# First transfers, second norm and last chunks reordered in a one-core encoder block

## The chip, the core and the metric

The kernel runs on one core of a Trainium2 chip. The metric is device microseconds of one execution. The core's engines run side by side, each in its own order of instructions, and wait for each other by semaphores: TensorE (PE in the profile; its weight loads are PEld), VectorE (DVE), ScalarE (ACT), GpSimd (POOL) and SyncE (SP), which issues nearly all transfers.

## The reference, cut to what matters

One layer over 1024 positions of width 1024, all in float32, with D_FF = 2816:

```python
h = rmsnorm(x, norm1_g);  proj = h @ w_in               # columns: q, k, v of group A, then of group B
ya = chunked_attention(qa, ka, va, rel_bias)            # 8 heads of 64
yb = stick_breaking_attention(qb, kb, vb)               # 8 heads of 64
x = x + concat(rmsnorm(ya, g_a), rmsnorm(yb, g_b)) @ w_out
x = x + conv_gated_mlp(rmsnorm(x, norm2_g), ...)        # up, causal conv of 3, silu(gate) * value, down
return rmsnorm(x, final_g)
```

## The kernel before, in words

Everything is held transposed: a tile is 128 channels by 1024 positions, so x is eight tiles (`KT = 8`), `xT[0]` to `xT[7]`. Every float32 product is made of three matmuls: each operand is split into a high part (rounded, type fp32r, made by ACT as a cast) and a low part (source minus high part, made by DVE or POOL), and `mm3` (L140) multiplies high by high, high by low and low by high. A matmul has at most 512 columns, so a tile is worked in two halves, `lo` and `hi` (`rows(0)`, `rows(1)`).

The order of PE is written out by hand for the whole kernel (`pe_order`). From the first value projection on, the order of SP, DVE, ACT and POOL is the order of the program text too (`loads_order`, `own_order`), partly by way of a small planner with costs (`Flow`). Before that point, the start stage leaves these four to a scheduler.

**Start (L203 to L269, L876 to L889).** Ten warm-up matmuls on zeros; then the first q and k projections (weights `w_in[12]` and `w_in[16]`) of all eight tiles. SP brings q's weights in two halves around the two halves of x's first tile, then x's second tile, k's weights, the other six tiles, and the first two v weights. For each tile, `enter` (L227) makes the scaled high part (`hTh`, ACT) and low part (`hTl`, DVE); `square` (L234) squares the tile in place, odd tiles on POOL, even ones on ACT, and DVE adds the squares into two sums. PE takes q of tile i and then k of tile i-1. The low and high half of a weight tile serve x's tiles 0 to 3 and 4 to 7. The sums are due after five steps of the v projection (`rstd`, `totals`).

**Second norm (L1176 to L1243, L1400 to L1440).** The output projection adds to `x2` (`paf` scales what PE made, L848; L852 adds), half 0 of all tiles and then half 1. While half 1 is made, `second_norm(0)` scales half 0 tile by tile (`scalar_tensor_tensor`, L1207), ACT casts (`h2h`, L1210), and DVE makes the low part (`h2l`). `totals` gives column sums of squares on PE (`n_ms`), `across` spreads them by transposes (`n_rb`). `up_first` then does the up-projection of the first channel tile plainly: sixteen groups of three matmuls on half 0 (`n` counts them), then eight tiles of half 1, two channel tiles each, in the order `K_ORDER[1]`. `norms[1]` is the same generator for half 1, advanced once at n = 5 (the totals) and once in each group from n = 8 (the transposes and the first tile). `weights1` splits the next weights; `combine_all` makes sums and differences of tiles (`t2`, `t3`, `t4`: Strassen-like products later). The bank of `u_a`, the first matmuls of the product for channel tile 3 (L1364), is emptied by an ACT copy at L1503, which stands behind the work for channel tiles 0 and 1 in ACT's order.

```python
if low:
    sub(*low.pop())                  # low part of the tile before
V.scalar_tensor_tensor(out=f, in0=f, scalar=c1(C_G2 + k), in1=ob, op0=ALU.mult, op1=ALU.mult)
S.copy(h, f)
low.append((l, f, h))
```

**Last chunks (`last_down`, L1757 to L1818).** The last two channel tiles of the down-projection are done for three groups of positions: 384, 384 and 256 columns (`LAST`). For each group and each of eight channel tiles: six matmuls (`dnl`), a DVE add into `x2` (L1808), a square (ACT, L1180 or L1185) with a POOL add into an accumulator (L1186). When a group is through, `final` is queued for it: the totals and the reciprocal root (`rn`), its transposes (`n_rb`), an ACT copy for POOL, and then eight scalings, of which POOL does those in `POOLD` or `POOLM` (ACT applies the gain to these beforehand, L1812) and DVE the others (L1783). `go(n)` advances it by n steps from within the next group's loop. The first two groups store each tile on its own (192 KB, L1787); the last one fills `res`, which leaves in two stores of 512 KB (L1818), after which the run ends.

## Time and profile before

| | us |
|---|---|
| median of 3 runs (lowest to highest) | 1247.58 (1245.27 to 1248.05) |
| the profiled execution, its own time | 1247.4 |
| its span, first to last instruction | 1245.6 |
| PE busy in the span | 1221.6 |
| DVE, ACT, POOL busy | 975.6, 633.8, 342.1 |
| granted TensorE clock, mean over the span | 0.994 |

The rows further down are single lines of the profile's views. In the timeline a row holds the start, the time covered, the engine, the line of the kernel, the operation, the tile written and the tiles read, the shape, the count (equal neighbours are merged), and in brackets how long the engine stood idle before it and what it waited for. Tiles of one name with other numbers are not told apart. A busy time of PE says little by itself, since matmuls overlap; the starts of neighbouring matmuls do.

### The profile page before, as it was taken

Reading aid. Unit: us, or ns where it says so; the run is one execution under the profiler, and the core shown is the slowest. Engines: PE = TensorE matmul, PEld = TensorE weight load, DVE = VectorE, ACT = ScalarE, POOL = GpSimd, SP = SyncE. Lnnn points to the kernel's source line nnn. Section 1 sums busy time; section 2 is a strip of 40 time slices with the busy share of each in tenths; the row PEclk is TensorE's granted clock in tenths of the full one; section 3 lists DMA queues with packets and bytes.
Section 4 is the critical chain, followed back from the end, with each engine's and each line's share of the span. In section 5 each row is a group of like instructions: output and inputs, shape, how many; then the busy total and the mean of one; then the engine's idle time right before and its main releaser. Section 6 shows DMA issues by size and latency. Waiting matters only on the chain.

```text
span 1245.6 us, 18039 instructions
## 1 busy us (share of the span) xinstructions
PE 1221.6 (98%) x6936; PEld 1031.8 (83%) x6936; DVE 975.6 (78%) x1403; ACT 633.8 (51%) x1072; POOL 342.1 (27%) x240
## 2 busy tenths in 40 slices
PE   8999999999999999999999999999999999999996
PEld 6989888988898788887778888888888887888886
DVE  7677788687676878557789888788787779969885
ACT  6345766665665756524455444444444445444434
POOL 3220113021312221242003443344344322132034
PEclk8999999999999999999999999999999999999998
DMA  5121122122302281234022212212212196430003
GB/s 223 34 56 31 59 61 93 28 77 77 86 18 60 53 243 69 86 103 151 1 85 102 102 70 83 102 68 85 101 69 85 53 380 243 158 113 1 1 1 135
DMA packets 39749, 113.47 MB, mean 91 GB/s; under 512 B 4720, under 2 KB 7920, under 8 KB 39664
## 3 DMA queue, kind: packets, MB, share of 16 engines
q1 hardware_dynamic: 39520, 112.22, 26.5%
q8 instruction: 54, 0.88, 0.3%
q14 instruction: 31, 0.25, 0.1%
q10 hardware_dynamic: 144, 0.11, 0.0%
HBM read 80.85 MB, written 24.12 MB: 84 GB/s over the span
## 4 chain that ended last, share of the span: by engine, by line
PE 83%; DVE 9%; ACT 4%; issue 2%; POOL 1%; DMA 1%; SPq 0%; DVEq 0%; ACTq 0%; POOLq 0%
PE u_a L1364 8%; PE u_e L1364 8%; PE dz L1879 8%; PE v_p L558 7%; PE q_p L143 6%; PE k_p L143 6%; PE u_c L1364 4%; PE u_b L1364 4%; PE u_d L1364 4%; PE pb L143 3%; PE dm L1879 3%; PE dj L1879 3%; PE pa L143 3%; PE yb L659 2%; PE tpb L645 2%; PE yy L774 2%
## 5 line engine op out<-in xcount | busy, mean ns | idle before, releaser
L622 DVE TENSOR_TENSOR_SCAN zb<-zb,first 128x128 f32<-128x128 f32 (+3 forms) x64 | 86.7, 1360 | 40.9 <-ACT zb L618 40.4
L558 PE MATMUL v_p<-v_h,hTh 128*128 128x256 f32 x256 | 74.2, 290 | 0.7 <-DVE k_f L435 0.7
L1388 DVE SCALAR_TENSOR_TENSOR gt<-cg,cst,gt 128x1023 f32<-128x1023 f32 (+1 forms) x44 | 74.0, 1681 | 0.8
L558 PE MATMUL v_p<-v_l,hTh 128*128 128x256 f32 x256 | 72.3, 283 | 0.0
L558 PE MATMUL v_p<-v_h,hTl 128*128 128x256 f32 x256 | 72.3, 282 | 0.0
L1254 POOL TENSOR_TENSOR up_r<-up_r 128x512 f32<-128x512 f32 x18 | 39.2, 2178 | 103.8 <-issue 92.5
L617 ACT ACTIVATE acts<-zb 128x127 f32<-128x127 f32 (+3 forms) x64 | 42.1, 658 | 43.6 <-PE zb L609 43.2
L649 ACT COPY tb<-tpb 128x512 f32<-128x512 f32 (+3 forms) x96 | 43.5, 483 | 33.2 <-PE tpb L645 32.9
L1388 DVE SCALAR_TENSOR_TENSOR vt<-cv,cst,vt 128x1023 f32<-128x1023 f32 (+1 forms) x44 | 57.7, 1311 | 1.5 <-ACT vt L1382 0.7
L143 PE MATMUL q_p<-hTh,q_h 128*128 128x512 f32 x128 | 53.0, 424 | 2.4 <-ACT hTh L229 2.4
L740 ACT ACTIVATE pa<-sa,sta 128x640 f32<-128x640 f32 (+4 forms) x64 | 42.3, 662 | 22.4 <-DVE sta L726 17.8
L121 POOL TENSOR_TENSOR q_l<-q_r,q_h 128x1024 fp32r<-128x1024 f32 x7 | 16.7, 2391 | 132.8 <-ACT q_h L416 132.8
L143 PE MATMUL k_p<-hTh,k_h 128*128 128x512 f32 x128 | 51.2, 410 | 0.0
L1382 ACT ACTIVATE vt<-cv,cst 128x1024 f32<-128x1024 f32 x22 | 27.4, 1245 | 45.9 <-DVE cv L1257 45.9
L143 PE MATMUL q_p<-hTl,q_h 128*128 128x512 f32 x128 | 49.7, 398 | 0.2
L558 PEld LDWEIGHTS v_p<-v_h,hTh 128*128 128x128 f32 x256 | 48.7, 190 | 1.2 <-DVE k_f L435 0.9
L143 PE MATMUL q_p<-hTh,q_l 128*128 128x512 f32 x128 | 49.3, 396 | 0.0
L143 PE MATMUL k_p<-hTh,k_l 128*128 128x512 f32 x128 | 49.2, 395 | 0.0
L143 PE MATMUL k_p<-hTl,k_h 128*128 128x512 f32 x128 | 49.2, 395 | 0.0
L558 PEld LDWEIGHTS v_p<-v_h,hTl 128*128 128x128 f32 x256 | 48.8, 191 | 0.3
L558 PEld LDWEIGHTS v_p<-v_l,hTh 128*128 128x128 f32 x256 | 48.8, 191 | 0.0
L625 DVE TENSOR_TENSOR acts<-zb,acts 128x127 f32<-128x127 f32 (+3 forms) x64 | 47.4, 749 | 1.2
(1265 smaller groups left out, 4042.2 us busy)
## 6 DMA issues: line engine op xcount, KB each, us to landing
up_r<-in_w_up_dram SPq DMA_DIRECT2D x44, 512.0 KB, 4.4
act<-vt SPq DMA_DIRECT2D x22, 512.0 KB, 2.6
dr<-in_w_dn_dram SPq DMA_DIRECT2D x20, 512.0 KB, 5.8
dr<-act SPq DMA_DIRECT2D x20, 512.0 KB, 6.6
k_r<-in_w_in_dram SPq DMA_DIRECT2D x8, 512.0 KB, 3.6
v_r<-in_w_v_dram SPq DMA_DIRECT2D x8, 512.0 KB, 4.1
spill<-yb SPq DMA_DIRECT2D x16, 256.0 KB, 2.0
wo_r<-in_w_out_dram SPq DMA_DIRECT2D x8, 512.0 KB, 3.7
```

Of the source, the lines that this page charges most:

```text
L143: PE.matmul(o, w[:, sl], t[:, rows(g)], start=first and i == 0, stop=last and i == 2,)
L558: PE.matmul(ov, a[k][:, cols(t)], b[:, sl], start=k == 0 and i == 0 and t4 % 2 == 0, stop=k == KT - 1 and i == 2, skip_group_check=True,)
L617: S.activation(a[:, 1:w], z[:, 1:], AF.Sigmoid)
L622: on_v(2 * w + 70, lambda: V.tensor_tensor_scan(out=z, data0=z, data1=first[:, :w], initial=0.0, op0=ALU.mult, op1=ALU.add)),
L625: on_v(w, lambda: V.tensor_tensor(out=a[:, 1:w], in0=z[:, : w - 1], in1=a[:, 1:w], op=ALU.mult)),
L649: mine.append(flow.add(on_s(m * P, lambda o=o, tp=tp: S.copy(o, tp))))
L740: on_s(w + 170, lambda: S.activation(po, full, AF.Exp, bias=st[:, 0:1], accum_out=st[:, 1:2])),
L1254: eng.tensor_tensor(out=out, in0=a, in1=b, op=ALU.subtract)
L1364: PE.matmul(o, w[:, cols(k)], t, start=start and k == 0 and i == 0, stop=k == 3 and i == 2, skip_group_check=True,)
L1382: S.activation(t, self.c[w], AF.Identity, bias=c1(C_CB + ct), scale=c1(C_W2 + ct))
L1388: V.scalar_tensor_tensor(out=t[:, : T - lag], in0=o[:, lag:], scalar=c1(c + ct), in1=t[:, : T - lag], op0=ALU.mult, op1=ALU.add,)
L1879: PE.matmul(o[m], w[:, cols(m)], t, start=i in (0, 1, 4, 5) and p == ps_[0] and j == 0, stop=p == ps_[-1] and j == 2, skip_group_check=True,)
```

## The change

At the start, transfers and engine work are written in order of first use: both orders by hand (`loads_order`, `own_order`) now begin here; q and k weights both come in halves, k's low half before x's second tile, both high halves behind it; PE takes q and k of the same tile; all squares are ACT's, three tiles late, and DVE's adds four tiles late; the v weights are brought and split before the last squares. In the second norm, the low part of a tile is made after the scaling of the next one, for half 0 and half 1; the steps of half 1 begin at n = 10 in place of 8, what is left of them is emitted ahead of PE's half 1, with the second part of `weights1` and three of the four steps of `combine_all("t2")`, which is a generator now. In the last chunks POOL's tiles are 2; 6 and 7; 2 and 4 for the three groups, the steps of `final` are called later, and the results leave in four stores of 256 KB.

```diff
--- before.py
+++ after.py
@@ -33,8 +33,7 @@
 CHUNKS = (range(5), range(5, 10))
 LAST = ((0, 3), (3, 6), (6, 8))
 ORDER_B = (7, 0, 6, 1, 5, 2, 4, 3)
-POOLD = (2, 6)
-POOLM = (2,)
+POOL_D = {3: (2,), 6: (6, 7), 8: (2, 4)}
 RATE_B, LEAD_B = 31.0, 8.0
 RATES_A, LEAD_A = (25.0, 25.0, 25.0, 21.0), 6.5
 LAG = 0.25
@@ -42,7 +41,8 @@
 SLACK = 0.6
 DRAIN = 1.6
 EARLY = 2
-SQ_LAG = 2
+SQ_LAG = 3
+ADD_LAG = 4
 WARM = 10
 TAIL_A = (6, 8, 4)
 X2_TAGS = ("h1", "l1", "h2", "l2", "x4", "x5", "h0", "l0")
@@ -215,14 +215,23 @@
             return weights(src, name, pool, tags, raw=work(tag, f"{name}_r"), bufs=bufs)
 
         halves = (slice(0, GW), slice(GW, T))
-        raw = work("wa", "q0_r")
-        pre = {12: (wp.tile([P, D], F32R, tag="wh", name="q0_h"), wp.tile([P, D], F32R, tag="wl", name="q0_l"))}
-        t0 = slot(0, "xin0")
-        nc.sync.dma_start(raw[:, halves[0]], w_in[12][:, halves[0]])
-        nc.sync.dma_start(t0[:, halves[0]], xT[0][:, halves[0]])
-        nc.sync.dma_start(t0[:, halves[1]], xT[0][:, halves[1]])
-        nc.sync.dma_start(raw[:, halves[1]], w_in[12][:, halves[1]])
-        hh, hl, sums, xin = [], [], [], []
+        lo, hi = halves
+        loads_order = tc.manual_schedule(engines={nc.sync.engine})
+        loads_order.__enter__()
+        own_order = tc.manual_schedule(engines={V.engine, S.engine, GP.engine})
+        own_order.__enter__()
+        pre, raw = {}, {}
+        for ct, name, tag in ((12, "q0", "wa"), (16, "k0", "wb")):
+            raw[ct] = work(tag, f"{name}_r")
+            pre[ct] = [wp.tile([P, D], F32R, tag=t, name=f"{name}_{t}") for t in ("wh", "wl")]
+        xin = [slot(k, f"xin{k}") for k in range(KT)]
+        hh, hl, sums = [], [], []
+
+        def bring(t, src, r):
+            nc.sync.dma_start(t[:, r], src[:, r])
+
+        def prepare(ct, r):
+            split(*(t[:, r] for t in pre[ct]), raw[ct][:, r])
 
         def enter(k, r):
             a, b, t = hh[k][:, r], hl[k][:, r], xin[k][:, r]
@@ -232,40 +241,50 @@
             )
 
         def square(k):
-            t = xin[k]
-            if k % 2:
-                GP.tensor_tensor(out=t, in0=t, in1=t, op=ALU.mult)
+            S.activation(xin[k], xin[k], AF.Square)
+
+        def add(k):
+            if k < 2:
+                sums.append(xin[k])
             else:
-                S.activation(t, t, AF.Square)
-            if k < 2:
-                sums.append(t)
-            else:
-                V.tensor_tensor(out=sums[k % 2], in0=sums[k % 2], in1=t, op=ALU.add)
-
+                V.tensor_tensor(out=sums[k % 2], in0=sums[k % 2], in1=xin[k], op=ALU.add)
+
+
+        bring(raw[12], w_in[12], lo)
+        bring(xin[0], xT[0], lo)
+        bring(xin[0], xT[0], hi)
+        bring(raw[16], w_in[16], lo)
+        nc.sync.dma_start(xin[1], xT[1])
+        bring(raw[12], w_in[12], hi)
+        bring(raw[16], w_in[16], hi)
+        for k in range(2, KT):
+            nc.sync.dma_start(xin[k], xT[k])
         for k in range(KT):
-            xin.append(slot(k, f"xin{k}") if k else t0)
-            if k:
-                nc.sync.dma_start(xin[k], xT[k])
             a, b = hpair(k, "hT")
             hh.append(a)
             hl.append(b)
             if k == 0:
-                split(pre[12][0][:, halves[0]], pre[12][1][:, halves[0]], raw[:, halves[0]])
-                enter(0, halves[0])
-                enter(0, halves[1])
-                split(pre[12][0][:, halves[1]], pre[12][1][:, halves[1]], raw[:, halves[1]])
+                prepare(12, lo)
+                enter(0, lo)
+                enter(0, hi)
+                prepare(16, lo)
             else:
                 enter(k, slice(0, T))
-            if k == 1:
-                pre[16] = preload(w_in[16], "k0", "wb")
+            if k == 3:
+                prepare(12, hi)
+                prepare(16, hi)
             if k >= SQ_LAG:
                 square(k - SQ_LAG)
+            if k >= ADD_LAG:
+                add(k - ADD_LAG)
+        pre[0] = preload(w_v[0], "v0_0", "wa", kp, ("y1", "y2"), 1)
+        pre[1] = preload(w_v[1], "v0_1", "wb", kp, ("x10", "x11"), 1)
         for k in range(KT - SQ_LAG, KT):
             square(k)
+        for k in range(KT - ADD_LAG, KT):
+            add(k)
         V.tensor_tensor(out=sums[0], in0=sums[0], in1=sums[1], op=ALU.add)
-        tc.keep_in_program_order(S.preload_act_table_set("sqrt_and_others"))
-        pre[0] = preload(w_v[0], "v0_0", "wa", kp, ("y1", "y2"), 1)
-        pre[1] = preload(w_v[1], "v0_1", "wb", kp, ("x10", "x11"), 1)
+        S.preload_act_table_set("sqrt_and_others")
 
         class Chain:
 
@@ -874,17 +893,12 @@
 
 
         oq, ok = (big(f"{w}0_p") for w in "qk")
-        for i in range(KT + 1):
-            for o, ct, k in ((oq, 12, i), (ok, 16, i - 1)):
-                if 0 <= k < KT:
-                    mm3(
-                        [o[:, rows(g)] for g in range(G)], *pre[ct], cols(k), hh[k], hl[k],
-                        k == 0, k == KT - 1,
-                    )
-        loads_order = tc.manual_schedule(engines={nc.sync.engine})
-        loads_order.__enter__()
-        own_order = tc.manual_schedule(engines={V.engine, S.engine, GP.engine})
-        own_order.__enter__()
+        for k in range(KT):
+            for o, ct in ((oq, 12), (ok, 16)):
+                mm3(
+                    [o[:, rows(g)] for g in range(G)], *pre[ct], cols(k), hh[k], hl[k],
+                    k == 0, k == KT - 1,
+                )
         fetch()
         fetch()
         v0 = project_v(0)
@@ -1202,12 +1216,12 @@
                 if g == 0:
                     hp2[k] = hpair(k, "h2", H2_TAGS.get(k))
                 f, (h, l) = x2[k][:, r], (t[:, r] for t in hp2[k])
-                if low:
-                    sub(*low.pop())
                 V.scalar_tensor_tensor(
                     out=f, in0=f, scalar=c1(C_G2 + k), in1=ob, op0=ALU.mult, op1=ALU.mult
                 )
                 S.copy(h, f)
+                if low:
+                    sub(*low.pop())
                 low.append((l, f, h))
                 if i == KT - 1:
                     sub(*low.pop())
@@ -1244,8 +1258,6 @@
     with stage("ffn"):
         fp = pools["sbuf"]
 
-        lo, hi = halves
-
         def at(slot, name, dt=F32):
             pool = wp if slot == "wr" else fp if slot[0] == "s" else cp
             return pool.tile([P, T], dt, tag=slot, name=name, bufs=1)
@@ -1344,6 +1356,7 @@
                 if low:
                     low()
                 low = nxt
+                yield
             low()
 
         def right(what, k):
@@ -1424,17 +1437,22 @@
                     if n == 5:
                         next(norms[1])
                         weights1(0)
-                    if 8 <= n:
+                    if n >= 10:
                         next(norms[1])
                     plain(o[0, ct], up_w[ct], k, 0, k == 0, k == KT - 1)
                     n += 1
                 S.copy(c[0][ct // NF][:, lo], o[0, ct])
+            for _ in norms[1]:
+                pass
+            weights1(1)
+            sums = combine_all("t2")
+            for _ in range(3):
+                next(sums)
             for i, k in enumerate(K_ORDER[1]):
                 for ct in (0, NF):
                     plain(o[1, ct], up_w[ct], k, 1, i == 0, i == KT - 1)
             for ct in (0, NF):
                 S.copy(c[0][ct // NF][:, hi], o[1, ct])
-            weights1(1)
             w2, raws2 = [], up_raw.pop(2)
 
             def weights2(n):
@@ -1453,20 +1471,23 @@
 
             done = Finish(0, *c[0])
             done.first("g")
+            for _ in sums:
+                pass
             done.first("v")
             low = weights2(0)
-            combine_all("t2")
             done.taps("g")
             done.taps("v")
             done.silu()
             low()
             done.gate()
-            combine_all("t3")
+            for _ in combine_all("t3"):
+                pass
             c[1] = (at("s7", "cg1"), at("s8", "cv1"))
             product_1(0, med)
             low = weights2(1)
             load_up(3)
-            combine_all("t4")
+            for _ in combine_all("t4"):
+                pass
             low()
             product_1(1, pj)
             load_up(4)
@@ -1773,8 +1794,8 @@
                 across(ob, rn2, c0, c_end)
                 rb = fp.tile([P, GW], F32, tag="eb", name=f"n3_{c0}_rbs", bufs=1)[:, :n]
                 S.copy(rb, ob)
-                pool_d = POOLD if c_end == KT else POOLM
-                for d in sorted(range(KT), key=lambda d: d not in pool_d):
+                pool_d = POOL_D[c_end]
+                for d in range(KT) if c_end == 6 else sorted(range(KT), key=lambda d: d not in pool_d):
                     x = x2[d][:, sl]
                     y = res[d // 4][:, d % 4, :] if c_end == KT else x
                     if d in pool_d:
@@ -1808,15 +1829,21 @@
                     V.tensor_tensor(out=x2[d][:, sl], in0=x2[d][:, sl], in1=o, op=ALU.add)
                     last = accs[: {3: 1, 6: 2, 8: 4}[c_end]]
                     x2_part(x2, d, sl, [a[:, sl] for a in last], None, f"n3_{c0}", sqs[d % 2][:, :GW])
-                    if d in (POOLD if c_end == KT else POOLM):
+                    if d in POOL_D[c_end]:
                         S.activation(x2[d][:, sl], x2[d][:, sl], AF.Copy, scale=c1(C_GF + d))
-                    if d > 0:
-                        go(2 if d == KT - 1 else 1)
+                    if c_end < KT:
+                        go((d > 1) + 2 * (d == KT - 1))
+                    elif d in (2, 3, 4):
+                        go(1)
                 todo.append(final(c0, c_end))
+            go(3)
+            next(todo[-1])
             go(20)
-            for i in range(2):
-                nc.sync.dma_start(outT[4 * i : 4 * i + 4, :, sl].rearrange("d p t -> p d t"), res[i])
-
+            for i in range(4):
+                nc.sync.dma_start(
+                    outT[2 * i : 2 * i + 2, :, sl].rearrange("d p t -> p d t"),
+                    res[i // 2][:, 2 * (i % 2) : 2 * (i % 2) + 2, :],
+                )
 
         first = up_first()
         load_up(5)
```

## Rows read from the trace of the kernel before

**Rows 1.** The page: busy time, share of the span and instructions of each engine

```profile
PE 1221.6 (98%) x6936; PEld 1031.8 (83%) x6936; DVE 975.6 (78%) x1403; ACT 633.8 (51%) x1072; POOL 342.1 (27%) x240
```

**Rows 2.** Windows: length, busy (count) of PE, PEld, DVE, ACT, POOL, clock, DMA share, GB/s

```profile
9.00:12.00 3.00, 1.38 (x3) 0.67 (x3) 1.70 (x3) 2.75 (x4) 0.13 (x1) 0.60 1.02 419
12.00:15.00 3.00, 3.00 (x8) 2.33 (x9) 3.00 (x2) 1.97 (x2) 2.67 (x1) 0.50 1.03 416
15.00:18.00 3.00, 3.00 (x12) 2.41 (x11) 3.00 (x3) 2.21 (x3) 0.97 (x1) 0.77 1.03 410
```

**Rows 3.** Timeline of PE, the start and the first v matmul

```profile
10.52 1.22 PE L143 MATMUL q_p<-hTh,q_h 128*128 128x512 f32 x2 [2.36 <-ACT hTh L229]
...
14.56 1.05 PE L143 MATMUL k_p<-hTl,k_h 128*128 128x512 f32 x2
...
19.08 0.62 PE L143 MATMUL q_p<-hTh,q_h 128*128 128x512 f32 x2
...
34.04 0.28 PE L558 MATMUL v_p<-v_h,hTh 128*128 128x256 f32 x1
```

**Rows 4.** Timeline of ACT and DVE, the start

```profile
8.38 1.05 ACT L239 ACTIVATE xin<-xin 128x1024 f32<-128x1024 f32 x1
...
10.50 1.28 DVE L230 SCALAR_TENSOR_TENSOR hTl<-xin,cst,hTh 128x1024 fp32r<-128x1024 f32 x1 [1.30 <-ACT hTh L229]
...
11.67 2.42 ACT L229 ACTIVATE hTh<-xin,cst 128x1024 fp32r<-128x1024 f32 x2 [0.24 <-DMA xin<-in_xT_dram]
...
23.19 2.91 DVE L230 SCALAR_TENSOR_TENSOR hTl<-xin,cst,hTh 128x1024 fp32r<-128x1024 f32 x1
```

**Rows 5.** Transfers issued at 2.13 and 2.61 us: KB, us from issue to landing

```profile
q_r<-in_w_in_dram SPq DMA_DIRECT2D x1, 256.0 KB, 5.7
...
xin<-in_xT_dram SPq DMA_DIRECT2D x1, 512.0 KB, 6.5
```

**Rows 6.** Timeline of PE, second norm and up-projection

```profile
576.38 0.50 PE L143 MATMUL pa<-yh,wo_h 128*128 128x512 f32 x1 [0.80 <-DVE paf L848]
...
586.35 0.50 PE L1416 MATMUL u<-h2h,up_h 128*128 128x512 f32 x1 [0.37 <-ACT h2h L1210]
...
588.79 0.62 PE L173 MATMUL n_rb<-ident,rn 128*128 128x128 f32 x4 [0.98 <-DVE rn L153]
...
600.79 0.50 PE L1416 MATMUL u<-h2l,up_h 128*128 128x512 f32 x1 [0.23 <-DVE h2l L121]
...
652.76 0.50 PE L1364 MATMUL u_a<-h2h,ua_3ph 128*128 128x512 f32 x1 [0.91 <-ACT cg L1503]
```

**Rows 7.** Timeline of DVE, the same stretch

```profile
591.88 0.69 DVE L121 TENSOR_TENSOR h2l<-x,h2h 128x512 fp32r<-128x512 f32 x1 [0.69 <-ACT h2h L1210]
...
609.50 0.69 DVE L121 TENSOR_TENSOR up_10pl<-up_r,up_10ph 128x512 fp32r<-128x512 f32 x1 [2.66 <-ACT up_10ph L124]
...
640.88 0.69 DVE L1257 TENSOR_TENSOR up_r<-up_r 128x512 f32<-128x512 f32 x1 [3.27 <-DMA up_r<-in_w_up_dram]
```

**Rows 8.** Line L121, 590 to 607 us: ns min/median/max, first and last start

```profile
L121 DVE TENSOR_TENSOR h2l<-x,h2h x8: 691/692/693, 591.9 to 606.2; 128x512 fp32r<-128x512 f32 x8
```

**Rows 9.** Windows: columns as in rows 2, the chain behind the second norm

```profile
609.50:637.60 28.10, 28.10 (x125) 23.28 (x124) 27.50 (x37) 16.73 (x25) 0.00 (x0) 1.00 0.14 42
```

**Rows 10.** Timeline of PE, DVE and SP, the last chunk

```profile
1230.68 3.84 PE L1804 MATMUL dnl<-lx,lw 128*128 128x256 f32 x30
...
1235.20 2.24 PE L160 MATMUL n_ms<-ones,n_acc 128*128 128x2 f32 x16 [0.68 <-DVE x2n L1783]
...
1238.92 2.44 DVE L1783 SCALAR_TENSOR_TENSOR res<-x2n,cst,n_rb 128x256 f32<-128x256 f32 x6 [0.98 <-ACT n_rbs L1775]
...
1240.25 1.55 SPq L1818 DMA_DIRECT2D out_dram<-res x2
```

**Rows 11.** Stores issued at 1241.4, and 1232 to 1238 us: KB, median us to landing

```profile
out_dram<-res SPq DMA_DIRECT2D x1, 512.0 KB, 3.3
...
out_dram<-x2n SPq DMA_DIRECT2D x8, 192.0 KB, 1.9
```

## The prediction

> **What bounds the kernel now.** I read the page first. TensorE (PE) is busy 98% of the span [rows 1], so time is to be had only where PE stands still or runs at its lower clock. The next view is therefore PE's own timeline, searched for idle time and for steps longer than the usual one. Three places stand out, and the change touches all three; the rest of the run (34 to 574 us and 655 to 1205 us) shows PE short waits only.
>
> *The start.* PE waits 2.36 us before 10.52 us for the high part of the second x tile [rows 3]. Around it the granted clock is at 0.50 of 2.4 GHz, that is at 1.2 GHz: the means of 0.60, 0.50 and 0.77 in three windows [rows 2] put the fall at 9.6 us and the rise at 16.4, and a pair of 512-column matmuls spans 1.05 us instead of 0.62 [rows 3]. From 19.08 to 34.04 us PE does 66 matmuls without a hole: 0.227 us a step. 96 matmuls make this block; at that step they take 21.8 us, and the block takes 28.3 (5.75 to 34.04).
>
> *The second norm.* PE waits 0.80, 0.37, 0.98 and four times 0.23 us (one of the four at 600.79) [rows 6], and the steps beside these holes are long too. The DVE rows tell why: each of the eight low parts of the second half starts only after its own ACT cast, so one tile takes 2.04 us (591.9 to 606.2 us is seven steps [rows 8]; each low part waits 0.69 us [rows 7]), while PE needs 6 x 0.227 = 1.36 us for a tile. After that PE waits 0.91 us more at 652.76 [rows 6].
>
> *The end.* The last totals (n_ms, 1235.20 us) wait for a DVE scaling of the chunk before; then DVE scales six results, and two stores of 512 KB end the run [rows 10].
>
> **The change part by part.** The sums are made against the profiled execution (1247.4 us, span 1245.6); it lies 0.2 us under the median 1247.58.
>
> *Start, transfers.* k's first half takes the place of q's second half as fourth transfer. The fourth was issued at 2.13 and landed 5.7 us later, at 7.8; the next (a whole x tile) was issued at 2.61 and landed at 9.1 [rows 5]. The order behind these changes, but the bytes ahead of the third x tile are the same, so that tile and all later ones land as before (the third: 11.65). PE then does: q of tile 0 until 8.1 as before; k of tile 0 from 8.5 (cast 0.6 after landing), low part of k at 9.2, done at 9.9; q of tile 1 from 10.3 (ACT enters tile 1 at 9.1, since no square is ahead of it now; that was 1.05 us at 8.38 [rows 4]); it waits 0.8 us for DVE's low part (1.28 us [rows 4]) at 11.5, and ends at 12.5. From there twelve matmuls a tile are 2.72 us; the low parts of tiles 2 to 7 are ready at 14.1, 15.4, 18.5, 20.5, 22.5 and 24.8 (ACT 1.15 and 1.05 us for each tile's entry and square; DVE 1.28 for the low part, 1.2 for an add), always ahead of PE, which ends at 30.2. That is 3.8 us earlier, if the clock stays up.
>
> All eight squares go to ACT. That adds four times 1.06 us there; ACT's queue then ends near 30 us, and nothing behind it is due before PE's totals at 37.5. GpSimd (POOL) no longer works here, so DVE's low part takes 1.28 us [rows 4] and not the 2.91 that it took beside POOL. DVE's last add ends near 34, also ahead of the totals; if all seven low parts took 2.91, that end would come 11 us later and PE would wait some 8 us there.
>
> The clock is the open term. Before, the longest hole was 2.36 us; now the holes are about 0.4, 0.4 and 0.8 us. If the lower level comes for the same stretch (9.6 to 16.4 us), PE ends at 32.6: a gain of 1.5. Bounds 1.5 and 3.8; I take **3.1**, nearer to the second since the largest hole shrinks to a third.
>
> *Second norm.* In each step DVE now scales tile k before it makes the low part of tile k-1, so ACT's cast (0.62 us) runs behind the next scaling. A step becomes 0.65 + 0.61 = 1.26 us of DVE, less than PE's 1.36. By places: (a) the wait of 0.80 at 576.38 ends with DVE's paf, which is queued behind the split of an up weight, whose ACT cast waits for the scaled tile; with the scaling first in the step that cast starts 0.6 us earlier: -0.65. (b) At 585.6 to 587.4 tiles 6 and 7 now come 1.4 us earlier: the two holes and the long steps, -1.0. (c) The wait for the transposed scale (0.98 at 588.79) goes, since its transposes stand two groups later (from the 9th to the 11th); what is late next is the low half of the second up weight, about 0.2: -0.95. The scaling of the second half still starts behind DVE's splits of the next weights, about 588.3 (before about 590.4, a scaling and a wait ahead of the 591.88 of [rows 7]). (d) With 1.26 us a tile it is done near 599; PE starts there at 591.8, ends 602.7 and finds every tile about 2 us ahead: -2.5. (e) The wait at 652.76 (0.91 and the long step behind it, -1.1) ends with an ACT copy that stands at the end of a DVE and ACT chain. That chain begins with the next weights' split, which DVE reached at 609.50 after 2.66 us of idleness [rows 7]; now it is emitted ahead of the PE group and begins near 599.5, some 10 us earlier, and it holds one outside wait (3.27 us for a transfer [rows 7]) that is issued by this same chain and so moves with it. PE arrives 5.1 us earlier, the chain 10: the wait goes. Sum -6.2, bounds: -3.5 ((a) to (d) at their bare holes, (e) nothing) and -6.6. I take **6.2**.
>
> Three steps of the t2 combination move ahead of the ACT copies of the banks; these copies then come at 608 as before, and PE needs those banks next at about 624.
>
> *End.* For the second chunk the totals move from the second to the third group: PE's 0.5 us wait for POOL goes, but the square root's table load (1.28 us of ACT) now comes later, and the transposes wait about as long: 0. In the last chunk seven scalings stood between the eight adds; now two do, three follow the last add, one comes after the reciprocal and two go to POOL. So PE sets the pace: its groups of six take 0.77 us or a little less (3.84 for thirty [rows 10]); eight of them from 1225.8, with 1.35 us of totals and 1.1 of transposes and waiting between, end at about 1234.0 (PE stopped at 1234.5 before, 1230.68 + 3.84, but the totals had to wait for DVE's scalings [rows 10]). The last add thus comes about 2.0 us earlier, the totals 1.6, since their sixteen short matmuls run behind each other, and DVE's last result 1.7, at about 1239.7 (1238.92 + 2.44 = 1241.36 before [rows 10]). POOL's two results (0.73 us each) start at once with ACT's copy and end at 1238.7: covered. The stores: before, issues at 1240.25 and 1241.4 [rows 10], and the second landed 3.3 us after its issue [rows 11], 4.5 after the first. The four new ones are issued at about 1238.1, 1238.6, 1239.0 and 1239.7. If bytes bound them, the last lands at 1238.1 + 4.5 = 1242.6; if the last issue does, at 1239.7 + 1.9 (a store of 192 KB [rows 11]) = 1241.6. Before it was 1244.7. Bounds 1.0 (the stores of the chunk before, which now lie closer ahead, delay them) and 3.0; I take **2.0**.
>
> Eight stores of 192 KB were issued between 1232 and 1238 us, and each landed 1.9 us after its issue on median [rows 11]: 15 us of stores in 6, so their fixed parts overlap. The Trainium skill, "DMA: Bandwidth & Descriptors", sections "Anatomy of one DMA" and "Bandwidth", says that a transfer pays a fixed part of about 2 us besides its bytes and that transfers should be batched to 1 MiB or more; by that rule alone four stores would be the worse choice. Where these fixed parts overlap, as in these rows, it costs nothing; where they don't, it is rival C.
>
> Total: 3.1 + 6.2 + 2.0 = 11.3; 1247.4 - 11.3 + 0.2 = **1236.3 us**.
>
> **The rivals.** *A: the middle gain is given back at 652.76.* If the DVE chain moves by less than PE does, PE waits there for what it won: only the start and the end remain, 1247.6 - 5.1 = 1242.5. For it: DVE is 27.5 of 28.1 us busy between 609.5 and 637.6 [rows 9], so it is that chain that leads. Against it: some 8 us of DVE idleness before it go (eight waits of 0.69 and the one of 2.66 [rows 7, 8]). *B: the start is not carried to the end,* because a wait between 34 and 574 us ends with something that doesn't move: 1239.4. Against it: all waits there end with ACT or DVE work on PE's own results. *C: the four stores run one behind the other,* 4 x 1.9 us from 1238.1, landing at 1245.7 instead of 1244.7: the end loses 1.0, 1239.3. *D, slower: PE stays at 1.2 GHz.* If holes spread over the start keep the clock down for longer than now, each matmul costs 0.2 us more. The whole gain (3.8 + 6.2 + 2.0 = 12.0) is gone after 60 of them; if the 84 of tiles 1 to 7 all ran so, the block would end at 45.8, 11.7 later than now, and the run take 1247.6 + 11.7 - 8.2 = 1251.1. Against it: at the lower level PE is the slower side and has no holes, and the clock rose at 16.4 after a stretch without any. *E: it does not do what it says:* the casts still bind each step (a tile's low part waits as before) and the end's scalings only move: 1247.6 - 3.1 - 1.0 = 1243.5.
>
> **How the numbers follow.** Forecast 0.62, A 0.12, B 0.08, C 0.05, D 0.03, E 0.05; the rest, 0.05, is several small losses that leave no change. The forecast's own range is 1234.0 to 1240.0 (gains 7.5 to 13.4). B and C lie in it, A just above; 1233.8 to 1242.2 leaves E, D, half of A and the rest out. A measurement tells 0.2% (2.5 us) from no change. Faster: forecast, A, B, C, E: 0.92. Same: 0.04. Slower: D and a little: 0.04.
>
> **What would show it.** Start: the first v matmul near 30 to 32.6 us, DVE's low parts all at 1.28, no clock below 1.0 (or only one short stretch). Second norm: the second half's low parts 1.26 to 1.4 us apart, no PE hole over 0.3 us between 576 and 655. End: three scalings right behind the last add, the four issues within 1.6 us of each other, the last landing about 3 us behind DVE's last result. The prediction is wrong if the first v matmul stands later than 33, if a hole of 2 us or more opens before the first u_a matmul, or if the last store lands 5 us or more after the last DVE result.

## The result, and the profile after the change

The changed kernel takes 1235.4 us (median, 1235.0 to 1236.5); the kernel before took 1246.9 beside it. The ratio is 0.991, with a 95% interval of 0.9893 to 0.9927: 9 to 13 us less. The forecast was 1236.3. The profiled execution took 1235.0 us (1247.4 before), its span is 1233.2 us (1245.6).

To see where the time went, the span is cut at six events that both traces hold: the landing of x's third tile, the first v matmul, the first `pa` matmul, the first `u_a` matmul, the first `dnl` matmul, and the last landing. Each number is a difference of two times in the trace; each column adds up to the time of the last landing, near the span's end.

| us | before | after | difference |
|---|---|---|---|
| start to landing of the third x tile | 11.65 | 11.07 | -0.58 |
| from there to the first v matmul | 22.40 | 18.65 | -3.75 |
| to the first `pa` matmul | 497.85 | 497.97 | +0.12 |
| to the first `u_a` matmul | 120.86 | 115.80 | -5.06 |
| to the first `dnl` matmul | 553.96 | 553.71 | -0.25 |
| to the last landing | 38.00 | 35.03 | -2.97 |

The page of the kernel after, busy time (its PE row stands against [rows 1]):

```profile
PE 1216.6 (99%) x6936; PEld 1030.8 (84%) x6936; DVE 972.8 (79%) x1403; ACT 637.6 (52%) x1078; POOL 332.5 (27%) x237
```

PE does the same 6936 matmuls and is busy 5 us less. So of the 12.4 us some 5 are matmuls that ran faster or overlapped more, and the rest are holes that went.

**The start.** Windows of the kernel after (columns as in [rows 2]; the clock is the third value from the right):

```profile
10.00:12.00 2.00, 1.41 (x6) 0.86 (x5) 0.94 (x1) 0.91 (x1) 0.00 (x0) 1.00 1.04 424
12.00:14.00 2.00, 2.00 (x10) 1.65 (x9) 1.72 (x2) 1.88 (x4) 0.00 (x0) 1.00 1.02 410
14.00:16.00 2.00, 2.00 (x11) 1.65 (x10) 2.00 (x3) 2.00 (x4) 0.00 (x0) 1.00 1.03 412
```

The granted clock stays at 1.00, which is 2.4 GHz; before it was at 0.50 here [rows 2]. PE's timeline after:

```profile
9.68 0.73 PE L143 MATMUL q_p<-hTh,q_wh 128*128 128x512 f32 x2 [0.20 <-ACT hTh L238]
11.00 0.73 PE L143 MATMUL q_p<-hTl,q_wh 128*128 128x512 f32 x2 [0.59 <-DVE hTl L239]
...
29.72 0.28 PE L577 MATMUL v_p<-v_h,hTh 128*128 128x256 f32 x1
```

Holes of 0.20 and 0.59 us stand where one of 2.36 was [rows 3]. The 0.59 is PE's last wait in this stretch, and it is a wait for the second x tile, which lands 2.6 us ahead of the third. So the new start hangs on the second tile: 21.26 to 21.29 us pass from its landing to the first v matmul in eight profiles with all of the new start, and the third tile's landing serves as the mark only because it keeps its distance.

**The second norm.** PE after:

```profile
571.98 0.50 PE L143 MATMUL pa<-yh,wo_h 128*128 128x512 f32 x1 [0.61 <-DVE paf L867]
...
583.48 0.50 PE L1429 MATMUL u<-h2h,up_l 128*128 128x512 f32 x1 [0.34 <-DVE up_l L121]
...
584.50 0.60 PE L173 MATMUL n_rb<-ident,rn 128*128 128x128 f32 x4
...
643.48 0.39 PE L1377 MATMUL u_a<-h2h,ua_3ph 128*128 128x512 f32 x1
```

The ACT copy that `u_a` waited for before is over well ahead of it, by 638.08:

```profile
637.02 1.06 ACT L1524 COPY cg<-u 128x512 f32<-128x512 f32 x2
```

The rows answer to [rows 6]: the wait for `paf` is still there, the transposes and `u_a` no longer wait, and a new wait of 0.34 stands at the second up weight's low part. DVE after:

```profile
568.33 0.68 DVE L121 TENSOR_TENSOR h2l<-x,h2h 128x512 fp32r<-128x512 f32 x1
570.09 1.23 DVE L121 TENSOR_TENSOR up_l<-up_r,up_h 128x1024 fp32r<-128x1024 f32 x1 [1.09 <-issue]
571.24 0.69 DVE L867 TENSOR_TENSOR paf<-pa,rba 128x512 f32<-128x512 f32 x1
...
586.75 0.69 DVE L121 TENSOR_TENSOR h2l<-x,h2h 128x512 fp32r<-128x512 f32 x1
587.36 0.74 DVE L1219 SCALAR_TENSOR_TENSOR x<-x,cst,n_rb 128x512 f32<-128x512 f32 x1
588.02 0.69 DVE L121 TENSOR_TENSOR h2l<-x,h2h 128x512 fp32r<-128x512 f32 x1
```

At 570.09 DVE has waited 1.09 us; the profile names no releaser ("issue"), but ACT's cast of that weight ends at 570.00, just ahead. This cast and what stands before it, first in the kernel before, then after:

```profile
569.60 1.30 POOL L1186 TENSOR_TENSOR n_at<-n_at,n_sq 128x512 f32<-128x512 f32 x1 [1.45 <-ACT n_sq L1185]
570.85 0.69 DVE L852 TENSOR_TENSOR x<-x,paf 128x512 f32<-128x512 f32 x1
573.36 1.04 ACT L124 CAST up_h<-up_r 128x1024 fp32r<-128x1024 f32 x1
```

```profile
565.59 1.61 POOL L1200 TENSOR_TENSOR n_at<-n_at,n_sq 128x512 f32<-128x512 f32 x1 [1.35 <-ACT n_sq L1199]
566.68 1.06 DVE L871 TENSOR_TENSOR x<-x,paf 128x512 f32<-128x512 f32 x1
568.96 1.04 ACT L124 CAST up_h<-up_r 128x1024 fp32r<-128x1024 f32 x1
```

DVE's add now runs beside POOL's, and both take longer. The point on term (a) below comes back to this.

From 586.75 on, low part and scaling alternate without a wait. The eight low parts, by line (ns, then first and last start):

```profile
L121 DVE TENSOR_TENSOR h2l<-x,h2h x8: 684/686/693, 586.8 to 595.1; 128x512 fp32r<-128x512 f32 x8
```

Seven steps take 8.35 us, six of 1.26 and the last, with no scaling left, of 0.77; before they took 14.3 [rows 8].

**The end.** Waits of the kernel before around the totals of the first two chunks, and ACT's table load between them, which the earlier rows do not show:

```profile
1217.86 0.83 PE L160 MATMUL n_ms<-ones,n_acc 128*128 128x2 f32 x6 [0.54 <-POOL n_acc L1186]
...
1218.54 1.28 ACT L152 ACT_TABLE_LOAD   x1
...
1220.36 0.43 PE L173 MATMUL n_rb<-ident,rn 128*128 128x128 f32 x2 [0.52 <-DVE rn L153]
...
1228.27 1.50 PE L160 MATMUL n_ms<-ones,n_acc 128*128 128x2 f32 x12 [0.72 <-POOL n_acc L1186]
```

PE, ACT, DVE and SP after, the same places and the last chunk:

```profile
1208.66 0.72 PE L160 MATMUL n_ms<-ones,n_acc 128*128 128x2 f32 x6
...
1209.01 1.28 ACT L152 ACT_TABLE_LOAD   x1
...
1210.84 0.54 PE L173 MATMUL n_rb<-ident,rn 128*128 128x128 f32 x3 [0.29 <-DVE rn L153]
...
1217.68 1.50 PE L160 MATMUL n_ms<-ones,n_acc 128*128 128x2 f32 x12
...
1223.27 1.95 PE L160 MATMUL n_ms<-ones,n_acc 128*128 128x2 f32 x16
...
1226.85 2.44 DVE L1804 SCALAR_TENSOR_TENSOR res<-x2n,cst,n_rb 128x256 f32<-128x256 f32 x6 [0.63 <-ACT n_rbs L1796]
...
1227.75 1.99 SPq L1843 DMA_DIRECT2D out_dram<-res  x4
```

The totals of both chunks no longer wait, and the last ones (1223.27, against 1235.20 with 0.68 of waiting in [rows 10]) don't wait for a scaling. The four stores, the first and the last of them by their issue (KB, us to landing):

```profile
out_dram<-res SPq DMA_DIRECT2D x1, 256.0 KB, 2.2
out_dram<-res SPq DMA_DIRECT2D x1, 256.0 KB, 2.9
```

They land at 1229.93, 1230.73, 1231.48 and 1232.22.

### The profile page after: what moved, and what is told of

It reads as the page before. It is cut to its first block, busy times and chain, and to the rows that moved or that the text cites. A ratio compares the mean times of both kernels' runs of the same rounds, so it can differ in the third digit from the quotient of the medians.

```text
span 1233.2 us, 18046 instructions
## 1 busy us (share of the span) xinstructions
PE 1216.6 (99%) x6936; PEld 1030.8 (84%) x6936; DVE 972.8 (79%) x1403; ACT 637.6 (52%) x1078; POOL 332.5 (27%) x237
## 4 chain that ended last, share of the span: by engine, by line
PE 90%; DVE 5%; ACT 2%; issue 1%; DMA 0%; SPq 0%; POOL 0%; DVEq 0%; ACTq 0%; POOLq 0%
PE u_a L1377 8%; PE u_e L1377 8%; PE dz L1906 8%; PE v_p L577 7%; PE k_p L143 6%; PE q_p L143 6%; PE u L1429 5%; PE u_d L1377 4%; PE u_c L1377 4%; PE u_b L1377 4%; PE pb L143 3%; PE dj L1906 3%; PE dm L1906 3%; PE pa L143 3%; PE yb L678 3%; PE tpb L664 2%
## 5 line engine op out<-in xcount | busy, mean ns | idle before, releaser
L121 POOL TENSOR_TENSOR q_l<-q_r,q_h 128x1024 fp32r<-128x1024 f32 x7 | 16.8, 2393 | 158.4 <-ACT q_h L435 158.4
L784 ACT COPY pta<-tpa 128x512 f32<-128x512 f32 (+3 forms) x80 | 37.3, 478 | 19.3 <-PE tpa L780 18.9
L143 PE MATMUL q_p<-hTh,q_h 128*128 128x512 f32 x112 | 46.9, 419 | 0.0
L143 PE MATMUL k_p<-hTh,k_h 128*128 128x512 f32 x112 | 45.8, 409 | 0.0
L143 PE MATMUL q_p<-hTh,q_l 128*128 128x512 f32 x112 | 43.9, 392 | 0.0
L143 PE MATMUL q_p<-hTl,q_h 128*128 128x512 f32 x112 | 43.9, 392 | 0.0
L143 PE MATMUL k_p<-hTh,k_l 128*128 128x512 f32 x112 | 43.9, 392 | 0.0
```

Of the source, the lines that this page charges most:

```text
L143: PE.matmul(o, w[:, sl], t[:, rows(g)], start=first and i == 0, stop=last and i == 2,)
```

## The experiments

Theory: three independent gains (start about 4 us in the profiled pair, second norm 5, end 3), each from the step that the prediction names. Rivals: a gain that is carried only together with the others; the clock alone at the start; the store count as a loss. No run takes the start's new orders of transfers, casts, adds and matmuls apart, nor POOL's tiles from the later steps in the end. The same cuts for every profile ("landing" is the third x tile's):

| us | landing | to first v | to `pa` | to `u_a` | to `dnl` | to the end | median run |
|---|---|---|---|---|---|---|---|
| before | 11.65 | 22.40 | 497.85 | 120.86 | 553.96 | 38.00 | 1246.3 to 1247.1 |
| start alone | 11.31 | 18.65 | 497.94 | 121.07 | 554.31 | 37.68 | 1244.0 |
| second norm alone | 10.93 | 21.65 | 497.92 | 116.65 | 553.69 | 37.67 | 1241.2 |
| end alone | 11.12 | 21.87 | 497.95 | 120.70 | 553.96 | 35.10 | 1242.9 |
| swap alone | 10.60 | 21.64 | 497.94 | 118.30 | 555.47 | 37.67 | 1243.2 |
| before, filled hole | 11.21 | 21.55 | 497.91 | 119.86 | 553.99 | 38.03 | 1245.0 |
| after | 11.07 | 18.65 | 497.97 | 115.80 | 553.71 | 35.03 | 1235.4 |
| after, again | 11.32 | 18.66 | 497.93 | 115.76 | 553.71 | 34.86 | 1235.3 |
| after, squares on POOL | 11.30 | 19.01 | 497.86 | 115.78 | 553.68 | 35.11 | 1235.5 |
| after, two stores | 11.26 | 18.64 | 497.96 | 116.63 | 553.69 | 35.58 | 1235.9 |
| after, eight stores | 10.13 | 18.68 | 497.93 | 115.76 | 553.69 | 35.25 | 1235.2 |
| after, casts apart | 11.94 | 18.65 | 497.91 | 114.67 | 553.69 | 35.11 | 1233.8 |
| after, five stores | 11.29 | 18.67 | 498.00 | 115.82 | 553.71 | 34.92 | 1235.2 |
| after, both | 12.10 | 18.64 | 497.91 | 114.68 | 553.71 | 34.93 | 1234.8 |

**The three parts alone.** Edits: the parts of the diff that touch the start (L203 to L269 and the q/k loop); the second norm, `combine_all` and `up_first`; `last_down`.

> The kernel before with the change of the start alone (order of the first transfers, all squares on ACT, adds later, k's tile in step with q's). Theory, from the two traces: the first v matmul comes 4.3 us earlier (29.7 for 34.0) and all that follows moves by as much, since no wait between 34 and 574 us ends with something fixed: 1246.9 - 4.3 = 1242.6. Rival 1 (the prediction's own term): 3.1 us, 1243.8. Rival 2 (the start is only carried because the later parts make room for it): the first v matmul is as early, but a wait at 576 to 655 us takes back what it brought: 1245 or more.

> The kernel before with the change of the second norm alone (scaling ahead of the low part of the tile before, eleventh group instead of ninth, next weights and three steps of t2 ahead of the second half's matmuls). Theory: u_a's first matmul comes 4.9 us earlier than in the kernel before, and the run is 4.9 us shorter: 1242.0. Rival (the prediction's term): 6.2 us, 1240.7, if the early start took away what this part could win at 576 us. Second rival: 0 to 2 us, if the chain of DVE that ends at u_a is late again without the start's change.

> The kernel before with the change of the end alone (which scalings go to POOL, when they are taken up, four stores of 256 KB). Theory, from the two traces: between the first dnl matmul and the last landing 2.9 us go: 1244.0. Rival (the prediction's term): 2.0 us, 1244.9; the 0.9 between them would then come from the parts before. The three parts together give 4.3 + 4.9 + 2.9 = 12.1 us if nothing is shared or given back; the changed kernel is 11.5 to 12.2 faster.

Measured ratios to the kernel before: start 0.9974 (0.9965 to 0.9983), second norm 0.9953 (0.9939 to 0.9967), end 0.997 (0.9959 to 0.9981), which is 3.2, 5.9 and 3.7 us. In the table each part changes its own columns. The start gains 3.0 to 3.75 us between landing and first v, and the stretch behind it is the same in all fourteen profiles (497.85 to 498.00): rival B falls. My expectation of 4.3 for it took the profiled pair for typical; the pair's landing differs by 0.58, and that execution before had the longest hole and the latest v matmul of the four profiles with that start. The second norm gains 4.2 in its profile, less than the 5.06 of the changed kernel. There PE's clock fell once; its windows:

```profile
582.00:584.00 2.00, 1.90 (x13) 1.57 (x13) 1.94 (x4) 1.33 (x4) 0.00 (x0) 1.00 0.81 242
584.00:586.00 2.00, 2.00 (x7) 1.52 (x7) 1.66 (x2) 1.10 (x2) 0.00 (x0) 0.64 0.99 332
586.00:588.00 2.00, 2.00 (x7) 1.48 (x6) 1.40 (x4) 1.62 (x3) 0.00 (x0) 0.51 0.92 358
```

Eight steps of 0.43 instead of 0.22 cost 1.7 us, and hid the wait for the second up weight. The profile of the two stores shows the same fall at 581.6 us and the same loss (116.63), the others of the changed kernel don't. The end gains 2.6 to 3.0. The three medians add to 12.8 us against the 11.2 of the ratio, within their intervals (each 1.1 to 1.7 us to either side).

**One edit of the second norm.**

```diff
-                if low:
-                    sub(*low.pop())
                 V.scalar_tensor_tensor(
                     out=f, in0=f, scalar=c1(C_G2 + k), in1=ob, op0=ALU.mult, op1=ALU.mult
                 )
                 S.copy(h, f)
+                if low:
+                    sub(*low.pop())
```

> The kernel before with one edit of the second norm alone: each step scales tile k before it makes the low part of tile k-1; the ninth group, the late split of the next weights and the late t2 stay. Theory: the steps are 1.26 us apart, the four waits of 0.23 us and the two at 586 us go, the wait of about 1 us at 588.8 stays (the transposes still come after the ninth group). The split of the next weights stands behind ACT's copies of the banks and so moves with PE's last matmul there, about 3 us; u_a keeps it: 1246.9 - 3 = 1243.9. Rival (the swap is all of it, the early emission is decoration): -4.9, 1242.0. Rival A of the prediction (what PE wins is given back at u_a, whose chain moves less): 1246 to 1247, with a wait of 2 us or more at u_a.

Measured: 0.9975 (0.9965 to 0.9984), 3.1 us. Its PE timeline at `u_a`:

```profile
646.28 0.39 PE L1416 MATMUL u<-h2h,up_1wl 128*128 128x512 f32 x1
648.48 0.50 PE L1364 MATMUL u_a<-h2h,ua_3ph 128*128 128x512 f32 x1 [1.81 <-ACT cg L1503]
...
649.86 0.63 PE L1364 MATMUL u_a<-h2h,ua_3pl 128*128 128x512 f32 x1
```

and its windows there:

```profile
646.00:648.00 2.00, 0.67 (x3) 0.21 (x2) 1.96 (x3) 2.00 (x4) 0.00 (x0) 1.00 0.00 0
648.00:650.00 2.00, 1.52 (x6) 1.21 (x7) 2.00 (x4) 2.00 (x5) 0.00 (x0) 0.91 0.00 0
650.00:652.00 2.00, 2.00 (x7) 1.54 (x6) 1.89 (x2) 2.00 (x4) 0.00 (x0) 0.50 0.21 84
```

The waits of 0.23 us go, as expected. But the wait at `u_a` doubles to 1.81 (0.91 in [rows 6]), and behind it the clock drops to 1.2 GHz for eight steps. So 2.56 us are won up to `u_a`, and 1.5 of them lost before `dnl` (555.47 for 553.96). The median's 3.1 is the theory's number, but the profile does not bear out its mechanism: there this stretch gives about 1 us, and the rest of the difference lies in the start, which the edit does not touch. Whether other executions lose less behind `u_a` is not shown. Rival A is real in this kernel: the chain of DVE and ACT that ends at `u_a` moves less than PE does. Without that wait PE would come to `u_a` 3.46 us sooner behind the first `pa` matmul than in the kernel before; the chain begins (the split into `up_10pl`) 3.45 sooner, 74.15 us for 77.60, but ends only 2.56 sooner. In the changed kernel it begins at 68.02, and `u_a` does not wait. From `pa` to `dnl` the changed kernel is 4.26 us faster than this one; the eleventh group and the early emission share them, and no run takes the two apart. That `u_a` no longer waits there fits the chain's earlier begin, which is what the emission changes; no run has the emission alone.

**The clock alone, at the start.** The hole before q's second tile is filled in the kernel before:

```diff
         for i in range(KT + 1):
+            if i == 1:
+                for _ in range(6):
+                    PE.matmul(warm, zero[:, :P], zero[:, :GW], start=True, stop=True)
```

> The kernel before with six more warm-up matmuls (zeros, bf16) put between q's first tile and q's second, into the hole that is 1.2 to 2.4 us long there. It tells the clock from the order of the transfers. Theory: the granted clock stays up at 10 to 16 us, and eight or nine steps of 0.43 us become 0.22, but what comes next is late: k's weights (low part at 12.9) and the low part of the third tile, which DVE makes beside GpSimd (2.9 us, done at 15.8). So only about 1.0 us of the start's 3.0 comes: 1246.0. Rival (the clock is all of it): the first v matmul at 30, 1244.0. Second rival (the fall has another cause than the hole): the clock falls all the same, 1247.0.

Measured: 0.9989 (0.998 to 0.9998), 1.4 us. PE's timeline:

```profile
7.85 1.47 PE L880 MATMUL warm<-zero 128*128 128x512 bf16 x6
10.11 0.73 PE L143 MATMUL q_p<-hTh,q_h 128*128 128x512 f32 x2 [0.79 <-ACT hTh L229]
...
15.39 0.73 PE L143 MATMUL q_p<-hTl,q_h 128*128 128x512 f32 x2 [0.95 <-DVE hTl L230]
```

```profile
9.00:12.00 3.00, 1.62 (x7) 0.78 (x6) 1.91 (x2) 2.76 (x4) 0.54 (x1) 1.00 1.03 421
12.00:15.00 3.00, 2.45 (x11) 1.69 (x9) 3.00 (x2) 1.54 (x2) 2.26 (x1) 1.00 1.02 414
```

The clock (second fence, windows) stays at 1.00, so in the old start the hole is what brings the fall. But from the landing to the first v matmul 21.55 us pass, 0.1 to 0.85 less than in the four profiles without the filler: PE, now faster, waits 0.95 us for a low part. Where the rest of the median's 1.4 comes from, one profile cannot show; its interval is 0.2 to 2.5 us. So in the old order the clock is worth little, since the data are late: most of the start's gain is the new order.

**Squares back on POOL.** The changed kernel, odd squares on GpSimd:

```diff
-            S.activation(xin[k], xin[k], AF.Square)
+            if k % 2:
+                GP.tensor_tensor(out=xin[k], in0=xin[k], in1=xin[k], op=ALU.mult)
+            else:
+                S.activation(xin[k], xin[k], AF.Square)
```

> The changed kernel with the odd squares of the first norm back on GpSimd. Theory: four low parts take 2.8 to 2.9 us instead of 1.28 beside it, 6.4 us more on DVE, of which some 3.3 are slack (the last low part ends at 24.2 and PE takes it at 27.5): the first v matmul comes 2 to 3.5 us later, at 32 to 33, and the run takes 1237.5 to 1239. Rival (the order of the transfers is all of it, the place of the squares is hidden): 1235.4, the first v matmul at 29.7 to 30.

Measured: 1235.45 us, no difference (0.9916 for 0.991). The theory fell; the rival holds. DVE does slow down beside POOL:

```profile
15.96 2.38 DVE L121 TENSOR_TENSOR k_wl<-k_r,k_wh 128x512 fp32r<-128x512 f32 x1
...
22.98 2.91 DVE L239 SCALAR_TENSOR_TENSOR hTl<-xin,cst,hTh 128x1024 fp32r<-128x1024 f32 x1
...
26.95 4.05 DVE L121 TENSOR_TENSOR v_l<-v_r,v_h 128x1024 fp32r<-128x1024 f32 x2
```

but in the new order the slow ones are mostly k's second half, the last low part and a v weight, nearly all with slack: the first v matmul stands 19.01 us behind the landing, 0.36 later. Moving the squares to ACT removed a contention that cost 0.36 us in this profile, beside the rest of the new start; which part of that rest makes the slack, no run tells.

**Two, eight and five stores** of the changed kernel's last megabyte (by SP; in the third, the last one by ACT). The lines show what takes the place of the four stores:

```diff
+            for i in range(2):          # two
+                nc.sync.dma_start(outT[4 * i : 4 * i + 4, :, sl].rearrange("d p t -> p d t"), res[i])
+            for d in range(KT):         # eight
+                nc.sync.dma_start(outT[d][:, sl], res[d // 4][:, d % 4, :])
+            for d, queue in ((6, nc.sync), (7, nc.scalar)):     # five: tiles 0 to 5 as in the change
+                queue.dma_start(outT[d][:, sl], res[1][:, d % 4, :])
```

> The changed kernel with its last results in two stores of 512 KB, as before the change, instead of four of 256 KB. Theory: bytes bind the last store, fixed parts overlap; the second store is issued at the same point (right behind DVE's last result) and lands 3.3 us later instead of 2.9, so the run is 0.4 us longer: 1235.8. Rival (each transfer pays a fixed part of its own, fewer are better): 1.0 to 1.5 us shorter, 1234.2. The four stores of the change would then cost and not pay.

> The changed kernel with its last results in eight stores of 128 KB. Theory: SP issues one in 0.5 us, so the eighth goes out at about 1230.9 us of the span instead of 1229.3, and lands 1.9 us later (1232.8): 0.6 us longer than with four, 1236.0. Rival 1 (only the last store's bytes count): it lands 1 us earlier, 1234.4. Rival 2 (fixed parts one behind the other): four more of them, 4 us or more, 1239 or more.

> The changed kernel with its last results in five stores: three of 256 KB and one of 128 KB issued by SP, the last of 128 KB issued by ACT. Theory: what ends the run is the issue of the last store (SP issues one in 0.5 us) and some 1.9 us behind it for 128 KB; ACT has nothing else to do, so the last issue stands right behind DVE's last result. From that result to the last landing 2.1 instead of 2.9 us: 0.8 us shorter than the changed kernel. Rival (the bytes of the megabyte bind): 2.9 us again, no change.

From DVE's last result to the last landing: 2.94 and 2.92 us with four stores, 3.37 with two, 3.31 with eight, 2.98 with five. The medians (1235.9, 1235.2, 1235.2) also hold the spread of the landing and, for two, the clock's fall, so the trace is the better measure. Two cost 0.43, as expected, eight 0.38 (0.6 expected). The five gained nothing. Its stores (KB, us to landing):

```profile
out_dram<-res SPq DMA_DIRECT2D x1, 128.0 KB, 3.0
out_dram<-res ACTq DMA_DIRECT2D x1, 128.0 KB, 2.7
```

The ACT store was issued at 1229.47, right behind DVE's last result at 1229.44, but landed at 1232.18: the bytes ahead of it bind, not its issue. With four stores the landings stand 0.74 to 0.80 us apart, on average 262144 bytes in 0.76 us, 344 GB/s. The Trainium skill, "DMA: Bandwidth & Descriptors", section "Specifications", gives about 358 GB/s as a core's share of HBM. The stores stay below that, but it is no limit in these traces: the loads at the start run at 410 to 424 GB/s, before [rows 2] and after. What holds the stores near 344 stays open. With eight, SP's issues (0.5 us each) bind. The two large ones end later, since the second can only go out with the last result and has the most bytes. The Trainium skill's rule of fewer, larger transfers (the same page, section "Bandwidth") rests there on loads that GpSimd issued; for these last stores, issued by SyncE, the trace shows the reverse, 3.37 us with two and 2.94 with four.

**A better version.** Two splits of up weights are pulled apart: the low part behind the next `paf` and add, and the second weight's ACT cast one tile earlier. (`first_weights` now makes the cast and returns the low part to be called later; its own lines are left out.)

```diff
                 flow.emit(x2_chains[d, g])
+                if g == 1 and d == 5:
+                    low_0()                          # sub of weight 0
...
                 if g == 1 and d == 4:
-                    first_weights(0)
-        first_weights(NF)
+                    low_0 = first_weights(0)         # now the cast alone
+                if g == 1 and d == 6:
+                    low_nf = first_weights(NF)
+        low_nf()
```

> The changed kernel with two splits of up weights pulled apart. The first one's ACT cast stays, its low part on DVE comes one step later, behind the next paf and add; the second one's cast goes one tile earlier on ACT, its low part stays. Theory: term (a) of the prediction, which came out at 0.2 of 0.65, failed because DVE waits 1.09 us for that cast with the paf behind it; now DVE does paf and add in that time, and PE's waits of 0.61 (paf), 0.11 (totals) and 0.34 (low part of the second weight) go with their long steps: from the first pa to the first u_a matmul 114.5 instead of 115.8 us, the run 1.2 us shorter than the changed kernel on the same chip. Rival (DVE is full there and not the order but its sum binds): the waits move to the next paf and the totals, 0 to 0.4 us.

> The changed kernel with both edits, the splits pulled apart and the five stores. Theory: they lie 550 us apart and share nothing, so their gains add: 2.0 us shorter than the changed kernel, about 1233.4. Rival (u_a's chain of DVE gives the first one back, as in the kernel with the swap alone): 0.8 shorter, 1234.6, with a wait of PE at u_a.

> The changed kernel as it is, on the same chip as the three versions of it: 1234.5 to 1236.5 us, as before. Theory on the spread: the first v matmul stands 18.65 us behind the landing of the third x tile, whatever that landing is (10.1 to 11.3 us so far); if it is off by more than 0.1 us from that, the start has another source of spread.

Measured on one chip: the changed kernel again 1235.3 (1235.0 to 1236.5), casts apart 1233.8 (1233.3 to 1234.8; ratio to before 0.9898, 0.9884 to 0.9911), both 1234.8. From `pa` to `u_a` 114.67 us pass with the casts apart, 1.09 less than in the changed kernel again; expected was 114.5. DVE no longer idles:

```profile
569.73 0.68 DVE L867 TENSOR_TENSOR paf<-pa,rba 128x512 f32<-128x512 f32 x1
570.45 1.08 DVE L871 TENSOR_TENSOR x<-x,paf 128x512 f32<-128x512 f32 x1
571.45 1.21 DVE L121 TENSOR_TENSOR up_wl<-up_r,up_wh 128x1024 fp32r<-128x1024 f32 x1
```

Both together give the same 1.1 in the trace (114.68); the stores add nothing, so the expected 2.0 was half wrong. The median of "both" lies higher than that of "casts apart"; its profiled landing was the latest of all, at 12.10. The version with the casts apart has the lowest median, though its interval overlaps that of the changed kernel again (0.9897 to 0.9924); that it is faster rests on the 1.09 us in the trace. The expected 18.65 us from landing to the first v matmul holds in all three and in the kernel again (18.64 to 18.67).

## Why the prediction was right, point by point

- **Start, 3.1:** right in size and mechanism, with the last wait (forecast 0.8 us, measured 0.59) for the second tile's low part, as the sum has it. With the clock up it put the first v matmul at 30.2 for a landing at 11.65; the rule 11.65 + 18.65 gives 30.3. The gain at an equal landing is 3.0 to 3.75, the upper bound (3.8) for the execution that the sum was made against. The lower bound, the clock at 1.2 GHz for as long as before, did not occur in any of nine profiles with the new start. Rivals B and D fall. That the transfers land as before held only within their spread: the pair's landing differs by 0.58.
- **Second norm, 6.2:** measured 5.06, at the middle of its bounds. By the steps around each wait, against the usual 0.22: (b) 1.2 for 1.0; (d) 2.4 for 2.5; (e) 1.2 for 1.1: the ACT copy is done 5.4 us ahead of `u_a`, so rival A falls. **(a) failed:** 0.2 of 0.65. Its step "that cast starts 0.6 us earlier" did not come. The low part is out of the way, 0.60 us, but DVE's add ahead of the cast takes 1.06 us where it took 0.69, since in the new order it falls beside POOL's accumulation (1.61 us for 1.30); the other adds that overlap it there take 0.90 to 1.07. Counted from that add's start, the cast comes at 2.28 us instead of 2.51, only 0.23 earlier, and from the cast to PE's matmul 3.02 us pass in both kernels. The term left the engine beside DVE out. DVE still waits for the cast with `paf` queued behind; with the casts apart, PE's wait of 0.61 goes. **(c) was mis-sized:** the transposes no longer wait, but what is late next, the second up weight, costs 0.34 and a long step, 0.6 in all, and not 0.2: 0.5 of 0.95. The rest is a wait of 0.11 at the totals and single steps 0.1 us longer than usual. So the sign "no PE hole over 0.3 us between 576 and 655" failed twice, at the two places of (a) and (c).
- **End, 2.0:** measured 2.97, at its upper bound. The mis-sized term is "second chunk: 0": its sum assumed that the table load comes later with the totals. It does not: it stands behind ACT's square and begins 11.8 us after the first `dnl` matmul in both kernels (1218.54 and 1209.01), and the transposes follow at 13.6 us in both. PE has done one group more by then, and waits 0.29 where it waited 0.54 and 0.52. So the last chunk's first matmul is 1.05 us earlier against the first `dnl` matmul, where the forecast had nothing. The last result is 1.5 earlier beyond that (1.7 forecast; the wait of 0.72 for the second chunk's totals is among it), and the stores give another 0.43 (0.3 by the forecast's numbers). Rival C falls: the landings overlap.
- **Sum:** 11.3 forecast, 11.2 by the ratio, 12.4 by the profiled spans. The two wrong sizes (-1.1 and +1.0) cancel, and that is luck: 0.9 us between the forecast of 1236.3 and the measured 1235.4 says less than the three parts do. The pair's extra 1.2 is 0.6 of landing, and the rest lies in the start of the execution before, with its long hole. The stated range (1234.0 to 1240.0) is not that of the parts' bounds, which add to gains of 6.0 to 13.4, that is 1234.2 to 1241.6; the result lies in both.

## What to carry to other kernels

Before a start is compared between two traces, measure it from an event that the program does not set, here a landing: between single executions the landing alone differed by up to 2 us, two thirds of what this start gains. When PE is sped up ahead of a chain on other engines, move that chain by at least as much, or part of the wait returns in one piece; a long wait can be paid twice, as a hole and as a slower clock behind it (1.81 us and 1.5 more in the kernel with the swap alone). And where a wait hangs on an in-order queue, ask two things: what the engine waits for with the wanted instruction behind it, and which other engine's work the new order puts beside the instructions ahead of it.

## What the runs showed of the hardware

- The landing of the third x tile varies from 10.13 to 12.10 us in fourteen executions of two starts with the same bytes ahead of it, and the first v matmul follows it at 18.64 to 18.68 us with the new order (19.01 with squares on POOL). This alone moves a run by up to 2 us. The spread enters with the fourth transfer: the third lands at 5.26 to 5.64 us, the fourth at 6.28 to 8.11.
- TensorE's clock fell to 1.2 GHz in or behind holes of 1.23, 1.66, 1.90, 2.36 (starts) and 1.81 us (`u_a`); it did not behind 0.95 (filled hole), nor behind 1.15 at `u_a` of the start alone. It also fell at 581 to 585 us in two profiles behind column totals and short waits only, and not in others of the same order; why is open. Behind the wait of 0.98 to 1.00 us for the transposes it fell in one of five profiles.
- In the changed kernel with squares on POOL, GpSimd's squares took 1.9 to 4.0 us beside DVE, the same operation each time; DVE's low parts beside them 1.7 to 2.9 for 1.28. In the second norm DVE's add of 512 columns took 1.06 us beside POOL's accumulation and 0.69 without it, the accumulation 1.61 for 1.30.
